# A two-layer encoder kernel: when layer two's skewed position bias is written, how layer one's down-projection ends, and how layer two's values start

## The chip, the cores and the metric

The kernel runs on one core of one Trainium2 chip. The metric is the device time of one execution in microseconds. Three runs of the kernel before the change took 2891.97, 2894.02 and 2900.52 us; their median, 2894.02, is the time before. One more execution was profiled.

## The reference, cut to what matters

There are 1024 prompt rows and 8 x 16 sample rows of width 1024: 1152 rows, nine token tiles of 128. Two layers follow each other, each an attention and a gated feed-forward network with a causal convolution. Layer one looks back two chunks of 64, with a T5 bias and sinks. Layer two looks back eight chunks; its keys and values come from layer one's output, and its bias is a table by clipped distance.

```python
def relclip_bias(table, qpos, kpos):
    d = jnp.clip(qpos[:, None] - kpos[None, :], -REL_CLIP, REL_CLIP) + REL_CLIP
    return table[:, d]

def conv_ffn(h, prev, w_up, conv_w, conv_b, w_down):
    u = h @ w_up
    ...
    a, g = jnp.split(y, 2, axis=-1)
    out = (jax.nn.gelu(g) * a) @ w_down
    return out, ue[:, T:]
...
        x = layer_norm(ALPHA * x + (1 + g_f) * f, ln_g[l, 1], ln_b[l, 1])
        if l == N_A_LAYERS - 1:
            kv = ((x * (1 + sc_kv) + sh_kv) @ w_kv_b).reshape(B, T, 2, N_HEADS_B, HEAD_DIM)
            k_b = kv[:, :, 0]
            v_b = kv[:, :, 1]
```

## The kernel before, in words

Every product is done as three matmuls of high and low halves. `wload` (L174 to L180) loads a weight tile of 128 x 1024 into a staging buffer of the ring `self.ws`, and `split` makes the two halves: ScalarE casts the high one (L161), GpSimd or VectorE subtracts for the low one (L172). They land in a slot of `self.wring`.

The order of the work in `build` is: `opening` (first modulation, first hidden rows, half of layer one's keys), `tables` (layer one's bias table, written to `ea`), `attention(0)`, `out_proj(0)`, `ffn(0)`, `attention(1)`, `out_proj(1)`, `ffn(1)`. The program is one stream; a scheduler puts each engine's instructions in an order by its own simulated times and the order in the text, and each engine then runs its queue strictly in that order. All transfers are issued by SyncE.

**The skewed bias.** A head's bias depends on the distance only. `skew` (L1339 to L1344) writes each head's table row 128 times behind itself into a buffer in device memory, so that a read with a row pitch one element short gives the shifted rows: `ska`, 3 MB, for layer one and `skb`, 6 MB, for layer two. For layer two, `tables_b` makes the table `eb` (a load, two steps on VectorE, a store) and `skew(1)` copies it in one transfer; both stand at the start of `down` for layer one. `skb` is first read in `attention(1)`.

**Up-projection** (`ffn`). Two pairs of weight tiles go plainly (`plain`); the other twenty through `spair`, seven half-size products per pair (L1188), evicted by ScalarE and VectorE (L1147 to L1155), convolved (`conv_row`, L1027), gated and written to `actD` (L1073 to L1075). In layer one background products (`ada`) run between.

**Down-projection** (`down`). Three groups of three token tiles, `GR = ((0, 1, 2), (6, 7, 8), (3, 4, 5))`. For each of 22 weight tiles `fetch` loads a weight tile and a piece of `actD` and splits both; then 18 matmuls (L1255) add into six banks. In layer one there are four weight slots and five staging buffers, two of which (`lng`, `lnb`) lie where the last gated rows stood. When a group's sums are complete, `evict` (L1268) multiplies them by the gate, and `tail` adds the residual (L1274) and calls `norm_tail`: statistics (L871 to L875), square root (L860), scaling (L902), eight transposes on TensorE (L912) into the banks of `TBG`, their eviction with an affine (L920, L924), a copy of the transposed rows (`zt`, L928) that is written to `hmD`, and the split into `H`, from which the next projections read. In layer two, `KEEP = 6` weight tiles of the last group are kept back and multiplied token tile by token tile, each tile ending by itself; in layer one all three tiles of a group end together.

**Layer two's keys and values** (`attention(1)`). `vproj` makes one quarter of the value columns for all nine tiles in the order `LV[1]`, each tile 24 matmuls (L303) in one of banks 0 to 3 in turn, evicted by ScalarE and VectorE (L353, L354) and written to `vH`. The first quarter comes first, then the keys (`kproj`, L291) with `rescale` between, then the three other quarters, then `load_hm`, which loads the nine tiles of `hmD` into a ring of three buffers (L811), scales them (L815) and splits them into `H` for the queries. The order of the values now:

```python
LV = ((0, 1, 2, 8, 3, 4, 5, 6, 7), (0, 1, 2, 6, 7, 8, 3, 4, 5))
```

`issue_after(ins)` adds an edge of issue order behind `ins`; it is used in `ada` (matmuls behind a matmul) and in `out_proj` (loads behind a load). `keep_in_program_order` pins an instruction behind everything that was traced on its engine before.

Of the kernel before, what the change touches and what calls it, by code (L numbers as in the profile page):

```python
# [16 lines left out]
NT = 9  # L17
# [18 lines left out]
KEEP = 6  # L36
# [10 lines left out]
EL = "p"  # L47
# [50 lines left out]
class Trunk:  # L98
# [187 lines left out]
    def mmT(self, w, out, s0, n):  # L286
        H = self.H
        i = 0
        for a, p in ((1, 0), (0, 1), (0, 0)):
            for k in range(8):  # L290
                self.nc.tensor.matmul(  # L291
                    out[:, 0:n], w[a][:, k * 128 : k * 128 + 128], H[:, p, k, s0 : s0 + n], start=i == 0, stop=i == 23
                )
                i += 1

# [43 lines left out]
    def vproj(self, l, q, banks, tmp):  # L339
        nc = self.nc  # L340
        w = [self.wload(self.I[("wv0", "wv1")[l]][q, i]) for i in range(2)]
        o0 = (896, 512)[l]
        cs = slice(q * 256, q * 256 + 256)
        for t in LV[l]:
            ps = self.bank(banks.next())
            self.mmX(ps, t * 128, w, 4, 256)
            hl, v = tmp.next()
            v = v[:, 0:256]
            ts = slice(t * 128, t * 128 + 128)
            if t < 8:  # L350
                h4 = hl[:, 0:512].rearrange("p (h i d) -> p h i d", i=2, d=64)
                p3 = ps[:, 0:256].rearrange("p (h d) -> p h d", d=64)
                nc.scalar.copy(h4[:, :, 0, :], p3)  # L353
                nc.vector.tensor_sub(h4[:, :, 1, :], p3, h4[:, :, 0, :].bitcast(F32))  # L354
                nc.sync.dma_start(
                    self.vH[l][ts, 4 * q : 4 * q + 4, :], hl[:, 0:512].bitcast(F32).rearrange("p (h d) -> p h d", d=128)
                )
            if t * 128 >= o0:
                nc.scalar.copy(v, ps[:, 0:256])
                nc.sync.dma_start(self.O[("va", "vb")[l]][t * 128 - o0 : t * 128 - o0 + 128, cs], v)  # L360
            if t == 8:
                nc.sync.dma_start(self.vS[l][:, cs], v)


    def attention(self, l, wk):
# [440 lines left out]
    def load_hm(self, ring, aff):  # L806
        nc = self.nc
        G, B = aff
        for t in range(NT):
            s = ring.next()  # L810
            nc.sync.dma_start(s, self.hmD[t])  # L811
# [179 lines left out]
    def ffn(self, l, xsrc, xdst, affs):  # L991
# [222 lines left out]
        for j in range(NPL, NFF):  # L1214
            spair(j)
        self.drain()
# [3 lines left out]
    def down(self, l, xsrc, xdst, affs):  # L1220
# [7 lines left out]
        if l == 0:  # L1228
            self.tables_b(F[:, 1152:3200])
            self.skew(1)  # L1230
# [62 lines left out]
        for gi, g in enumerate(GR):  # L1293
            keep = KEEP if l and gi == 2 else 0
# [36 lines left out]
    def tables_b(self, t):  # L1331
# [5 lines left out]
        nc.sync.dma_start(self.eb, t)  # L1337

# [113 lines left out]
    def build(self):  # L1452
# [4 lines left out]
        self.tables()  # L1457
        self.attention(0, wk)
# [138 lines left out]
```

## Time and profile before

| | |
|---|---|
| median of 3 runs | 2894.02 us (2891.97 to 2900.52) |
| profiled execution, its own time | 2892.5 us |
| its span, first to last instruction | 2890.7 us |
| granted TensorE clock, mean | 0.973 |
| moved by DMA | 471.15 MB, mean 163 GB/s |

How to read it: the profile gives busy time for each engine, the waits of an engine with what ended them, the chain of waits that ended last, and, for any stretch, busy time, granted clock and share of the DMA engines. `L1188` is line 1188 of the kernel before. A row of waits reads: the waiting engine, what it writes and its line, `<-` who ended the wait, then total us, number of waits, the longest. A row of a timeline reads: start, duration, engine, line, operation, output and inputs, count, and in brackets the idle time ahead of it and what ended that. `SPq` is SyncE's queue, where a row is the issue of a transfer and not the transfer itself. PE is TensorE, ACT ScalarE, DVE VectorE, POOL GpSimd.

### The profile page before, as it was taken

How to read it: one execution, taken by the hardware profiler on the slowest of the kernel's cores; microseconds unless marked ns; L12 is line 12 of the kernel's file. 1: busy time of each engine (PE TensorE's matmuls, PEld its weight loads, DVE VectorE, ACT ScalarE, POOL GpSimd, SP SyncE). 2: the span in 40 equal slices, each digit the busy share in tenths (PEclk: the TensorE clock that was granted, in tenths of full speed). 3: DMA queues.
4: the chain of work that ended last, by engine and by line, in shares of the span. 5: the costliest groups of instructions: out<-in, count | busy, mean ns of one | idle time of the engine just before them, and what ended most of it. 6: DMA issues, size and time to landing. Idle time of an engine off the chain costs nothing.

```text
span 2890.7 us, 47351 instructions
## 1 busy us (share of the span) xinstructions
PE 2725.0 (94%) x17734; PEld 2425.9 (84%) x17734; DVE 1805.0 (62%) x3674; ACT 1296.9 (45%) x2613; POOL 1157.0 (40%) x761
## 2 busy tenths in 40 slices
PE   7999899999999959998999899979999999998997
PEld 5887678899999948887899788857899999997886
DVE  4477777876667743562112667767788778884763
ACT  3476634433333333543324666653454444453442
POOL 2122424444444435655731121232354443447662
PEclk8999899999999979999999899989999999999999
DMA  8655454434444374664865356675432222247561
GB/s 298 207 164 167 134 176 164 159 133 156 141 143 139 129 228 168 232 212 161 279 230 177 106 150 177 173 234 165 153 133 69 85 72 77 69 146 231 200 210 70
DMA packets 221062, 471.15 MB, mean 163 GB/s; under 512 B 39616, under 2 KB 115600, under 8 KB 220832
## 3 DMA queue, kind: packets, MB, share of 16 engines
q1 hardware_dynamic: 220832, 468.13, 49.5%
q8 instruction: 139, 2.28, 0.3%
q14 instruction: 91, 0.75, 0.1%
HBM read 366.74 MB, written 110.74 MB: 165 GB/s over the span
## 4 chain that ended last, share of the span: by engine, by line
PE 80%; DMA 8%; DVE 5%; ACT 3%; issue 2%; POOL 2%; SPq 0%; POOLq 0%; DVEq 0%; ACTq 0%
PE PS L1188 31%; PE PS L1255 17%; PE PS L291 11%; PE PS L303 10%; PE PS L587 2%; PE PS L565 2%; PE PS L218 2%; PE PS L537 1%; PE PS L540 1%; DMA actD<-F 1%; DMA F<-in_wdn_dram 1%; DMA ws<-in_wo_dram 1%; DVE F L504 1%; PE PS L912 1%; POOL H L172 1%
## 5 line engine op out<-in xcount | busy, mean ns | idle before, releaser
L1255 PE MATMUL PS<-wh,xa 128*128 128x512 f32 x1128 | 359.0, 397 | 40.6 <-ACT wh L161 40.6
L1188 PE MATMUL PS<-H,wh 128*128 128x256 f32 (+1 forms) x2560 | 394.2, 296 | 0.0
L1188 PEld LDWEIGHTS PS<-H,wh 128*128 128x128 f32 x2560 | 360.3, 190 | 0.0
L1248 DVE TENSOR_TENSOR xa<-xa 128x384 fp32r<-128x384 f32 x132 | 185.7, 1419 | 238.0 <-ACT xa L161 238.0
L172 POOL TENSOR_TENSOR wl<-ws,wh 128x1024 fp32r<-128x1024 f32 x87 | 216.8, 2495 | 291.5 <-ACT wh L161 277.5
L161 ACT CAST wh<-F 128x512 fp32r<-128x512 f32 (+1 forms) x249 | 176.0, 713 | 347.4 <-PE PS L1188 139.7
L1150 DVE TENSOR_TENSOR F<-PS,F 128x320 f32<-128x320 f32 (+2 forms) x600 | 192.5, 351 | 164.7 <-PE PS L1188 161.3
L291 PE MATMUL PS<-H,wh 128*128 128x384 f32 (+1 forms) x1536 | 294.8, 338 | 0.0
L1255 PEld LDWEIGHTS PS<-wh,xa 128*128 128x128 f32 x1128 | 213.3, 189 | 93.5 <-ACT wh L161 41.5
L291 PEld LDWEIGHTS PS<-H,wh 128*128 128x128 f32 x1536 | 267.4, 188 | 1.5 <-issue 1.0
L161 ACT CAST wh<-ws 128x1024 fp32r<-128x1024 f32 (+1 forms) x175 | 146.8, 843 | 247.9 <-PE PS L1188 99.7
L1027 DVE SCALAR_TENSOR_TENSOR F<-F 128x1024 f32<-128x1024 f32 x320 | 249.7, 822 | 6.4 <-ACT F L1066 5.3
L1188 PE MATMUL PS<-H,wl 128*128 128x256 f32 (+1 forms) x1280 | 228.1, 298 | 5.2 <-ACT F L1155 5.2
L172 DVE TENSOR_TENSOR wl<-F,wh 128x512 fp32r<-128x512 f32 x196 | 196.8, 1012 | 46.2 <-ACT wh L161 45.6
L1255 PE MATMUL PS<-wl,xa 128*128 128x512 f32 x564 | 224.8, 399 | 0.2 <-POOL wl L172 0.2
L1188 PEld LDWEIGHTS PS<-H,wl 128*128 128x128 f32 x1280 | 189.4, 190 | 12.2 <-issue 5.8
L1188 PE MATMUL PS<-xa,wh 128*128 128x256 f32 (+1 forms) x1280 | 196.1, 295 | 0.6 <-DVE xa L172 0.6
L303 PE MATMUL PS<-wh,H 128*128 128x256 f32 (+1 forms) x936 | 171.3, 313 | 11.2 <-DVE H L172 4.0
L1036 POOL TENSOR_TENSOR F<-F 128x16 f32<-128x16 f32 x88 | 45.1, 513 | 339.6 <-DVE F L1027 256.7
L1188 PEld LDWEIGHTS PS<-xa,wh 128*128 128x128 f32 x1280 | 178.7, 188 | 1.4 <-DVE xa L172 1.0
L172 POOL TENSOR_TENSOR wl<-F,wh 128x1024 fp32r<-128x1024 f32 x53 | 130.4, 2463 | 91.7 <-ACT wh L161 89.5
L1255 PE MATMUL PS<-H,xa 128*128 128x512 f32 x684 | 161.6, 395 | 1.9 <-POOL H L172 1.9
(245 smaller groups left out, 5686.3 us busy)
## 6 DMA issues: line engine op xcount, KB each, us to landing
F<-in_wdn_dram SPq DMA_DIRECT2D x71, 512.0 KB
ws<-in_adaw_dram SPq DMA_DIRECT2D x64, 512.0 KB
ws<-in_wdn_dram SPq DMA_DIRECT2D x61, 512.0 KB
ws<-in_wup_dram SPq DMA_DIRECT2D x50, 512.0 KB
actD<-F SPq DMA_DIRECT2D x44, 576.0 KB
xa<-actD SPq DMA_DIRECT2D x132, 192.0 KB
F<-in_adaw_dram SPq DMA_DIRECT2D x48, 512.0 KB
F<-in_wup_dram SPq DMA_DIRECT2D x38, 512.0 KB
```

The lines of the kernel that those rows point to most:

```text
L161: nc.scalar.copy(out, in_)
L172: self.eng(el).tensor_sub(lo, src, hi.bitcast(F32))
L218: mm = nc.tensor.matmul(ps[32 * j : 32 * j + 32, hf * 256 : hf * 256 + 256], self.cT[:, k * 32 : k * 32 + 32], w[:, j * 256 : j * 256 + 25 ...
L291: self.nc.tensor.matmul(out[:, 0:n], w[a][:, k * 128 : k * 128 + 128], H[:, p, k, s0 : s0 + n], start=i == 0, stop=i == 23)
L303: self.nc.tensor.matmul(out[:, 0:n], H[:, p, j * kn + k, t0 : t0 + 128], w[a][:, k * n : k * n + n], start=i == 0, stop=i == 23,)
L565: nc.tensor.transpose(t[:, n * 128 : n * 128 + 128], p[:, (kt - k0) * 128 : (kt - k0) * 128 + 128], self.ident)
L587: mm = nc.tensor.matmul(ob[:, i0 * 128 : (i0 + n) * 128], vst[a][:, kt, :], pp[:, m * 128 : (m + n) * 128], start=cnt == 0, stop=cnt == to ...
L1027: nc.vector.scalar_tensor_tensor(o, u, cw[:, cc, i : i + 1], o, op0=ALU.mult, op1=ALU.add)
L1150: nc.vector.tensor_add(d, o, x)
L1188: nc.tensor.matmul(ps[:, 0:m], w[a][:, k * 128 : k * 128 + 128], x(p, k, n), start=start and c == 0, stop=c == 11, skip_group_check=True,)
L1248: nc.vector.tensor_sub(lo, raw, hi.bitcast(F32))
L1255: nc.tensor.matmul(ps, a[p][:, i * 128 : i * 128 + 128], w[q][:, hf * 512 : hf * 512 + 512], start=j == 0 and c == 0, stop=j == NFF - 1 an ...
```

## The change

1. `tables_b` is called in `build` right behind `tables`, ahead of `attention(0)`, in another buffer. `skew(1)` is gone; a new function `skew_b` copies one head, and `ffn` calls it behind each of the first sixteen `spair`s of layer one.
2. In `down`, `KEEP` becomes `(4, 6)`: layer one too keeps weight tiles of its last group back, four of them. It gets two more weight slots, in `X2`; in its last group the transposed rows go to `zt` and `lnb` in turn, and the scaled rows to `hf` and `F[:, 0:1024]` in turn.
3. `vproj` takes several quarters and a cut: it loads all their weights, then makes the tiles of `LV` ahead of the cut for each quarter, then the tiles behind it. Layer two starts with quarters 0 and 1 and a cut of six (tiles 0, 1, 2, 6, 7, 8 first); quarters 2 and 3 follow the keys.
4. `mmT` remembers its last matmul, and `load_hm` issues its loads inside `issue_after` of it.

```diff
-KEEP = 6
+KEEP = (4, 6)
...
@@ mmT
-                self.nc.tensor.matmul(
+                mm = self.nc.tensor.matmul(
...
+        self.lastmm = mm.ins
@@ vproj (the body of the loop over tiles becomes vtile)
+    def vproj(self, l, qs, banks, tmp, cut=NT):
+        ws = [[self.wload(self.I[("wv0", "wv1")[l]][q, i]) for i in range(2)] for q in qs]
+        for part in (LV[l][:cut], LV[l][cut:]):
+            for q, w in zip(qs, ws):
+                for t in part:
+                    self.vtile(l, q, t, w, banks, tmp)
@@ attention
-        self.vproj(l, 0, kvb, kvt)
         if l == 0:
+            self.vproj(0, (0,), kvb, kvt)
             self.skew(0)
         else:
+            self.vproj(1, (0, 1), kvb, kvt, 6)
...
-            for q in range(1, 4):
-                self.vproj(1, q, kvb, kvt)
+            self.vproj(1, (2,), kvb, kvt)
+            self.vproj(1, (3,), kvb, kvt)
@@ load_hm
-            nc.sync.dma_start(s, self.hmD[t])
+            with self.tc.issue_after(self.lastmm):
+                nc.sync.dma_start(s, self.hmD[t])
@@ ffn
         for j in range(NPL, NFF):
             spair(j)
+            if l == 0 and 2 <= j < 18:
+                self.skew_b(j - 2)
@@ down
-        if l == 0:
-            self.tables_b(F[:, 1152:3200])
-            self.skew(1)
...
-        if l:
+        if l == 0:
+            order += [(self.X2[:, o : o + 1024], self.X2[:, o + 1024 : o + 2048]) for o in (0, 2048)]
+        else:
...
-        hfr = Ring([self.hf])
+        hfr, hfe, zts = Ring([self.hf]), Ring([self.hf, F[:, 0:1024]]), Ring([self.zt, self.lnb])
...
-                self.norm_tail(t, row, xdst, aff, True, Ring(TBG[gi]), "a", None, None, hfr, EL, VA)
+                if gi == 2:
+                    self.zt = zts.next()
+                self.norm_tail(t, row, xdst, aff, True, Ring(TBG[gi]), "a", None, None, (hfr, hfr, hfe)[gi], EL, VA)
...
-            keep = KEEP if l and gi == 2 else 0
+            keep = KEEP[l] if gi == 2 else 0
@@ skew_b (new)
+    def skew_b(self, h):
+        src = self.eb[h : h + 1, :]
+        self.nc.sync.dma_start(
+            self.skb[h : h + 1, :].rearrange("h (q w) -> h q w", w=768),
+            bass.AP(src.tensor, src.offset, [[768, 1], [0, 128], [1, 768]]),
+        )
@@ build
         self.tables()
+        self.tables_b(self.F[:, 8192:9472])
         self.attention(0, wk)
```

More of the change, by code (lines that the diff above doesn't have):

```diff
@@ L342, in vproj @@
         o0 = (896, 512)[l]
         cs = slice(q * 256, q * 256 + 256)
[L344 to L362, printed above, removed]
+        ps = self.bank(banks.next())
@@ new lines, in vtile @@
+        self.mmX(ps, t * 128, w, 4, 256)
+        hl, v = tmp.next()
+        v = v[:, 0:256]
+        ts = slice(t * 128, t * 128 + 128)
+        if t < 8:
+            h4 = hl[:, 0:512].rearrange("p (h i d) -> p h i d", i=2, d=64)
+            p3 = ps[:, 0:256].rearrange("p (h d) -> p h d", d=64)
+            nc.scalar.copy(h4[:, :, 0, :], p3)
+            nc.vector.tensor_sub(h4[:, :, 1, :], p3, h4[:, :, 0, :].bitcast(F32))
+            nc.sync.dma_start(
+                self.vH[l][ts, 4 * q : 4 * q + 4, :], hl[:, 0:512].bitcast(F32).rearrange("p (h d) -> p h d", d=128)
+            )
```

9 lines of the change are left out of this document (7 added, 2 removed).

## The prediction

> **What bounds the kernel now.** I read the page first, then the waits of TensorE over the whole span, then the chain of waits, and last the timelines of the two stages that the change touches.
>
> ```profile
> span 2890.7 us, 47351 instructions
> PE 2725.0 (94%) x17734; PEld 2425.9 (84%) x17734; DVE 1805.0 (62%) x3674; ACT 1296.9 (45%) x2613; POOL 1157.0 (40%) x761
> PE 80%; DMA 8%; DVE 5%; ACT 3%; issue 2%; POOL 2%; SPq 0%; POOLq 0%; DVEq 0%; ACTq 0%
> ```
>
> TensorE is busy for 2725.0 of 2890.7 us, and the change removes no matmul. What it can win lies in the 165.7 us in which TensorE stands still, and in matmuls run at a lower clock. So I looked for TensorE's single long waits.
>
> ```profile
> PE PS L1255 <- ACT wh L161: 40.6, 2, 33.4
> ```
>
> ```profile
> PE PS L912 <- ACT F L928: 8.9, 1, 8.9
> PE PS L912 <- DVE F L902: 5.2, 1, 5.2
> PE PS L303 <- POOL H L172: 3.2, 2, 2.1
> ```
>
> The first row (whole span) has one wait of 33.4 us, at the start of layer one's down-projection. The three others are all that TensorE waits for between 1330 and 1400 us, the seam between layer one's down-projection and layer two's value projection: 17.3 us. Together 50.7 us, and both places are edited.
>
> Why the 33.4 us: the issue queue of SyncE, the size of one transfer in the DMA list, and SyncE's own waits.
>
> ```profile
> 1047.40 0.60 SPq L1342 DMA_DIRECT2D skb<-eb  x1
> 1048.13 6.88 SPq L1075 DMA_DIRECT2D actD<-F  x1
> ...
> 1071.72 14.12 SPq L176 DMA_DIRECT2D F<-in_wdn_dram  x3
> ```
>
> ```profile
> skb<-eb SPq DMA_DIRECT2D x1, 6144.0 KB
> ```
>
> ```profile
> SPq L176 <- DMA actD<-F: 9.4, 1, 9.4
> ```
>
> At 1047.40 the skewed bias of layer two goes out as one transfer of 6144 KB. The last gated activation is issued right behind it, and the fourth and fifth weight tile may be loaded only when that write has left its buffer: at 1071.72. So the copy takes about 1071.7 - 1048.1 = 23.6 us, and TensorE waits for all of it and the loads behind.
>
> **The change part by part.**
>
> *The copy leaves the down-projection.* What is then late is the same chain without the copy: gate, write of the activation, weight load, cast. Layer two runs this stage without such a copy, and this is all that TensorE waits for from 2580 us to the end:
>
> ```profile
> PE PS L1255 <- ACT wh L161: 7.2, 1, 7.2
> PE PS L1255 <- POOL H L172: 1.9, 1, 1.9
> PE PS L1255 <- POOL wl L172: 0.2, 1, 0.2
> ```
>
> I take 7.2 + 1.9 = 9.1 us for what stays: gain 33.4 - 9.1 = 24.3 us. Ends: 29 (two more weight slots shorten the chain) and 17 (the residue nearly doubles). The stall also leaves TensorE slow behind it:
>
> ```profile
> 1048.00:1072.00 24.00, 1.65 (x8) 0.99 (x6) 2.66 (x2) 1.56 (x2) 5.32 (x3) 0.61 0.98 315
> 1072.00:1084.00 12.00, 0.91 (x2) 0.81 (x3) 0.56 (x1) 2.38 (x3) 0.89 (x1) 0.50 0.77 224
> 1084.00:1100.00 16.00, 16.00 (x63) 12.70 (x63) 4.90 (x2) 4.35 (x7) 9.53 (x5) 0.89 0.45 152
> ```
>
> ```profile
> 1083.09 98.36 PE PS L1255 x412
> ...
> 1197.60 78.87 PE PS L1255 x338
> ```
>
> In the windows the last three columns are granted clock, DMA share and GB/s: the clock is 0.50 in the stall and 0.89 in the 16 us behind it. In the chain the 412 matmuls behind the stall take 98.36/412 = 0.2387 us each, later ones 78.87/338 = 0.2333: 412 x 0.0054 = 2.2 us, gone with a short stall. Ends 1 and 3.
>
> *The seam (17.3 us).* Today all three tiles of the last group end together. Value tiles and the end's transposes share accumulator banks 0 and 1, so only value tiles in banks 2 and 3 may go first, and of these only two need none of the three ending tiles. Then TensorE stands behind transposes whose evictions stand behind something else:
>
> ```profile
> 1361.59 0.82 SPq L811 DMA_DIRECT2D F<-hmD  x2
> ```
>
> ```profile
> 1368.66 3.18 ACT L815 ACTIVATE F<-F,C 128x128 f32<-128x128 f32 x8 [5.61 <-DMA F<-hmD]
> 1371.75 0.28 ACT L860 ACTIVATE C<-C 128x1 f32<-128x1 f32 x2
> 1371.93 3.17 ACT L815 ACTIVATE F<-F,C 128x128 f32<-128x128 f32 x8
> ```
>
> ```profile
> 1387.59 8.89 PE PS L303 x72
> ```
>
> ScalarE's in-order queue holds the scaling of two tiles loaded far ahead (L815), and waits 5.61 us for their load while the square roots (L860) that the end needs stand behind it. The change answers in three ways. (a) Four weight tiles are kept back and each token tile ends by itself: 24 matmuls x 0.2333 = 5.6 us apart, so two of the three ends run while TensorE still multiplies. (b) Two column quarters start together: by the ring of four banks six value tiles lie in banks 2 and 3, not two, and a value tile is 24 matmuls, 8.89/3 = 2.96 us: 17.8 us of cover in place of 5.9. (c) The loads of L811 are placed inside an order edge behind the last key matmul. I count (c) as nothing: as I read it, the edge binds only instructions of that matmul's own engine, and these are loads on SyncE; every use in the kernel today pairs instructions of one engine. So the 5.61 us wait and 2 x 3.2 us of scaling may still stand ahead of the last tile's evictions. Today the first transposes start 5.9 + 5.2 = 11.1 us behind the last matmul, with three tiles sharing VectorE; for the last tile alone I estimate 8. L815 can add 5.61 + 2 x 3.2 = 12: 20 us against 17.8 us of cover leaves 2, and I add 2 for transposes queued a little early. I take 4 of 17.3: gain 13. Ends 16 and 7. Keeping weights back: layer two already keeps six, and the rows above hold no wait for it; 0, bound 3. The first two value weights are split later than now, since their slots carry kept tiles until the last token tile: 1 us, the 1.9 us row being the nearest bound.
>
> *Where the copy goes.* It is traced inside the up-projection, one head (1/16 of 6144 KB, 23.6/16 = 1.5 us) per pair of weight tiles. But each piece depends only on the small table, which is now built in the opening, and this schedule issues what is ready:
>
> ```profile
> L993 SPq DMA_DIRECT2D F<-in_cw_dram x2: 383/460/537, 257.0 to 1824.5; - x2
> ```
>
> ```profile
> 485.39 10.88 PE PS L291 x62
> ```
>
> The convolution weights are the first statement of this very up-projection, whose first matmuls start at 485.39, and they are issued at 257.0, as soon as their buffer is free. The pieces need no buffer. I expect all 16 right behind the table, from about 60 us, where layer one's twin of this copy stands today (last fence of the rivals). There the DMA engines look so (windows from 60 us):
>
> ```profile
> 60.00:75.00 15.00, 12.73 (x104) 12.52 (x102) 0.85 (x2) 2.44 (x5) 2.40 (x1) 1.00 1.03 351
> 75.00:85.00 10.00, 8.48 (x58) 8.49 (x59) 1.70 (x4) 2.81 (x6) 2.37 (x1) 0.83 0.60 210
> 85.00:95.00 10.00, 10.00 (x79) 10.00 (x79) 1.70 (x4) 1.86 (x5) 0.00 (x0) 1.00 0.98 290
> 95.00:106.00 11.00, 11.00 (x65) 11.00 (x64) 2.22 (x4) 2.73 (x7) 0.58 (x4) 1.00 0.83 223
> 106.00:140.00 34.00, 32.57 (x251) 28.09 (x249) 20.78 (x69) 20.88 (x65) 5.33 (x7) 1.00 0.49 156
> ```
>
> ```profile
> 76.52 0.78 PE L303 MATMUL PS<-wh,H 128*128 128x256 f32 x4 [3.79 <-DVE X L354]
> ...
> 106.21 0.22 PE L537 MATMUL PS<-xa 128*128 128x128 f32 x1
> ```
>
> Layer one's own bias copy fills 60 to 75 us, and already costs TensorE 3.79 us, through key writes queued behind it. Up to 106 us, when layer one's scores begin, the free part of the DMA engines is 10 x 0.40 + 10 x 0.02 + 11 x 0.17 = 6.1 us. If all 23.6 us of pieces run ahead of the keys, values and queries that the scores need, these come 23.6 - 6.1 = 17.5 us later, and TensorE has nothing else to do. Bounds: 0 if the pieces fall behind the start, where half of 34 us is free; 24 if they lead entirely. Some will slip behind the start, so I take 15. The table's two DVE steps and two small transfers join the opening; they are inside this bound.
>
> If the pieces do stay in the up-projection they cost nothing: TensorE's waits from 535 to 1000 us are 4 us in all, none on a transfer, the longest being
>
> ```profile
> PE PS L1188 <- ACT F L1155: 2.3, 1, 2.3
> ```
>
> *Sum*, on the profiled execution (2892.5 us): -24.3 - 2.2 - 13 + 1 + 15 = -23.5: 2869.0. That execution lies 1.5 us under the median of the runs (2894.0), so 2870.5 for the median, told as 2870.
>
> **The rivals.** *The pieces cost little* (under 8 us): the scheduler keeps them behind the keys and values, or where they are written. For it: 17 us of DMA time are free between 106 and 140 us, and the order of issue favours earlier program text among what is ready. Against: L993's 257.0. Sum with 0: 2854.0, 2855.5 for the median.
>
> *Slower: the pieces land one by one ahead of layer one's first keys.* A small write from the table's twin shows how long one landing takes:
>
> ```profile
> 55.41 0.33 SPq L1329 DMA_DIRECT2D ea<-F  x1
> ```
>
> ```profile
> 59.06 0.85 SPq L1342 DMA_DIRECT2D ska<-ea  x1
> ```
>
> The copy at 59.06 waits for the table issued at 55.41: 3.65 us. Sixteen such landings, each awaited before the next, are 58 us in place of 23.6; less the 6.1 us of room, 52. Against it: the order of issue runs several transfers deep. With the other terms as above the sum is 2892.5 - 38.5 + 52 = 2906, and 2907.5 for the median. It decides for slower once the opening loses over 38.5 + 8.7 = 47 us. The Trainium skill, page "DMA: Bandwidth & Descriptors", section "Anatomy of one DMA", speaks against cutting a copy up: each DMA on the GpSimd path pays some 2.0 us besides its bytes over 436 GB/s, by which an estimate for 16 pieces is 16 x 2.9 = 46 us, 40 less the room, and a total of about 2895; the page states this for another path than SyncE's, and no run here shows it yet.
>
> *Nothing to see*: the seam's ends slip behind the early scaling all the same (gain 7 or less), the residue nearly doubles (gain 17) and the opening pays 24: 2892.5 - 17 - 1 - 7 + 24 + 1 = 2892.5, 2894 for the median.
>
> **How the numbers follow.** Chances: forecast 0.60, little cost 0.24, slower 0.08, nothing to see 0.08. A measurement of this kernel can tell about 0.3%, 8.7 us. Of the forecast's 0.60, opening and seam both near their bad ends (-38.5 + 24 + 6) leave under 8.7 us in about 0.08; so faster 0.76 (0.52 + 0.24), same 0.15, slower 0.09, the last from the slower case and a little of the third. The range reaches down past the cheap case, 2853, and up to where the opening pays 24 and the seam gives 7: 2892.5 - 24.3 - 2.2 - 7 + 1 + 24 + 1.5 = 2885.5, told as 2887.
>
> **What would show it.** Right: in the changed profile the copy is 16 issues of skb from one line, the last well before 257 us; TensorE's first scores (L537) come 10 to 20 us later than 106; TensorE's longest wait in layer one's down-projection is 5 to 14 us; between the last down-projection matmul and the keys TensorE waits under 7 us in all, the loads of hmD still early. Wrong: the 16 issues lie between 535 and 1000 us, or the first scores come as before (then the cheap case); a wait over 17 us remains at the start of the down-projection though the copy is gone, which would mean that the activation write and not the copy was the cause; or the seam keeps a wait of 9 us on L928.

## The result, and the profile after

The changed kernel takes 2885.70 us (median of 11 runs, 2880.89 to 2890.38); the kernel before took 2895.64 us in the runs beside it (11 runs, 2888.97 to 2901.74). The ratio is 0.9966, with a 95% interval of 0.9953 to 0.998: some 10 us faster. The forecast was 24 us. The time lies inside the range, close to its upper end.

The profiled execution spans 2885.9 us. The longest wait of TensorE over the whole span:

```profile
PE PS L1264 <- ACT wh L161: 25.9, 2, 18.7
```

The line numbers have moved: L1255 is now L1264, L303 is L304, L537 is L544, L1188 is L1196, L912 is L920, L1074 is L1082, L354 is L360, L504 is L511, L811 is L819, L928 is L936. In the kernels of the experiments they move by another line or two. The wait of 33.4 us at the start of layer one's down-projection has become 18.7, not 9.1; the rest of the 25.9 is layer two's, as before.

The seam (all waits of TensorE from 1330 to 1400 us) has 6.2 us where 17.3 stood:

```profile
PE PS L920 <- DVE C L881: 3.2, 1, 3.2
PE PS L920 <- ACT F L936: 2.7, 2, 1.7
PE PS L304 <- DVE X L360: 0.3, 1, 0.3
```

The pieces of the skewed bias went out in the opening, between 68.8 and 117.5 us (one row by tile, then SyncE's issue queue, then TensorE):

```profile
L1352 SPq DMA_DIRECT2D skb<-eb x16: 470/602/2400, 68.8 to 117.5; - x16
```

```profile
82.55 1.78 SPq L1352 DMA_DIRECT2D skb<-eb  x3
84.44 0.53 SPq L361 DMA_DIRECT2D vH<-X  x1
85.02 5.89 SPq L1352 DMA_DIRECT2D skb<-eb  x7
```

```profile
83.52 0.80 PE L304 MATMUL PS<-wh,H 128*128 128x256 f32 x2 [5.39 <-DVE X L360]
...
114.06 0.28 PE L544 MATMUL PS<-xa 128*128 128x256 f32 x1
```

```profile
505.64 10.88 PE PS L291 x62
```

The first scores come at 114.06 in place of 106.21, and the up-projection's first chain at 505.64 in place of 485.39: the 7.9 us lost by the first scores have grown to 20.3.

For all kernels below I read the same milestones in the timeline of TensorE: the first scores, the first and last matmul of layer one's pair tiles, the last matmul of its down-projection, layer two's first scores, the first and last of its pair tiles, the last matmul. Stage lengths in us:

| kernel | to first scores | attention 1 to pairs | pairs 1 | down 1 | seam, keys, values | attention 2 to pairs | pairs 2 | down 2 |
|---|---|---|---|---|---|---|---|---|
| before | 106.2 | 428.5 | 502.3 | 318.1 | 239.8 | 538.2 | 454.0 | 288.8 |
| before, second profile | 106.2 | 430.7 | 503.2 | 318.8 | 237.7 | 545.9 | 455.6 | 289.3 |
| after | 114.1 | 440.9 | 504.3 | 302.8 | 224.9 | 541.1 | 455.4 | 287.6 |
| after, second profile | 118.8 | 435.0 | 501.5 | 303.3 | 226.3 | 540.8 | 455.8 | 287.7 |
| move_only | 117.1 | 438.0 | 501.7 | 302.6 | 237.9 | 539.1 | 456.6 | 286.7 |
| move_again | 116.0 | 445.6 | 504.4 | 301.1 | 235.2 | 534.6 | 453.1 | 287.8 |
| seam_only | 104.5 | 430.7 | 501.0 | 324.2 | 226.0 | 541.5 | 454.8 | 288.3 |
| stage | 119.7 | 436.4 | 503.5 | 282.5 | 223.8 | 541.5 | 453.9 | 288.0 |
| pin | 106.7 | 438.0 | 507.2 | 303.0 | 225.3 | 538.7 | 454.2 | 287.7 |
| late_table | 106.2 | 433.7 | 511.1 | 303.5 | 226.0 | 537.1 | 454.5 | 288.7 |
| whole | 132.1 | 434.2 | 503.9 | 303.9 | 226.8 | 541.7 | 455.3 | 287.4 |
| keep0 | 118.8 | 442.0 | 502.8 | 302.7 | 228.2 | 541.3 | 455.4 | 287.9 |
| one_quarter | 115.0 | 444.2 | 501.9 | 304.1 | 229.0 | 535.7 | 455.0 | 287.5 |
| held | 114.3 | 448.2 | 502.0 | 305.3 | 246.3 | 543.2 | 455.0 | 287.7 |
| pin_stage | 109.6 | 429.1 | 507.2 | 282.5 | 227.5 | 541.3 | 455.4 | 291.7 |
| pin_stage2 | 107.3 | 426.8 | 509.1 | 282.6 | 227.3 | 538.8 | 454.1 | 277.2 |
| pin_down | 108.4 | 429.1 | 504.6 | 290.8 | 225.9 | 538.3 | 453.2 | 277.5 |

In the three kernels with two profiles, the pair tiles and the down-projections mostly repeat within 2 us and always within 3.5. The two attentions don't: the two profiles of the kernel before differ by 7.7 us in layer two's attention alone, with the same instructions. A difference of a few us there is not told by one profile.

### The profile page after: what moved, and what is told of

Same layout as the page of the kernel before. It is cut to its first block, busy times and chain, and to the rows that moved or that the text cites. A ratio compares the mean times of both kernels' runs of the same rounds, so it can differ in the third digit from the quotient of the medians.

```text
span 2885.9 us, 47364 instructions
## 1 busy us (share of the span) xinstructions
PE 2728.5 (95%) x17734; PEld 2425.8 (84%) x17734; DVE 1816.1 (63%) x3674; ACT 1295.1 (45%) x2613; POOL 1159.7 (40%) x761
## 4 chain that ended last, share of the span: by engine, by line
PE 77%; DMA 9%; DVE 6%; issue 3%; ACT 2%; POOL 2%; SPq 1%; POOLq 0%; DVEq 0%; ACTq 0%
PE PS L1196 31%; PE PS L1264 18%; PE PS L291 10%; PE PS L304 8%; PE PS L594 2%; PE PS L572 2%; PE PS L218 2%; PE PS L544 1%; DMA ws<-in_adaw_dram 1%; DVE F L511 1%; PE PS L547 1%; DMA F<-in_adaw_dram 1%; PE PS L920 1%; PE PS L713 1%; DMA skb<-eb 1%
## 5 line engine op out<-in xcount | busy, mean ns | idle before, releaser
L1196 PE MATMUL PS<-H,wh 128*128 128x256 f32 (+1 forms) x2560 | 396.0, 297 | 0.0
L1196 PEld LDWEIGHTS PS<-H,wh 128*128 128x128 f32 x2560 | 362.2, 191 | 0.0
L172 POOL TENSOR_TENSOR wl<-ws,wh 128x1024 fp32r<-128x1024 f32 x78 | 193.6, 2487 | 313.7 <-ACT wh L161 302.1
L161 ACT CAST wh<-F 128x512 fp32r<-128x512 f32 (+1 forms) x236 | 162.4, 694 | 332.3 <-PE PS L1196 144.6
L1264 PE MATMUL PS<-wh,xa 128*128 128x512 f32 x864 | 279.2, 400 | 25.9 <-ACT wh L161 25.9
L291 PE MATMUL PS<-H,wh 128*128 128x384 f32 (+1 forms) x1536 | 294.4, 337 | 0.0
L291 PEld LDWEIGHTS PS<-H,wh 128*128 128x128 f32 x1536 | 267.2, 188 | 1.4 <-issue 0.6
L161 ACT CAST wh<-ws 128x1024 fp32r<-128x1024 f32 (+1 forms) x166 | 137.4, 831 | 238.8 <-PE PS L1196 97.6
L1196 PE MATMUL PS<-H,wl 128*128 128x256 f32 (+1 forms) x1280 | 229.1, 299 | 5.2 <-ACT F L1163 5.2
L1264 PEld LDWEIGHTS PS<-wh,xa 128*128 128x128 f32 x864 | 164.1, 190 | 66.5 <-ACT wh L161 26.8
L1196 PEld LDWEIGHTS PS<-H,wl 128*128 128x128 f32 x1280 | 190.1, 191 | 12.2 <-ACT F L1163 5.6
L1196 PE MATMUL PS<-xa,wh 128*128 128x256 f32 (+1 forms) x1280 | 196.1, 295 | 0.6 <-DVE xa L172 0.6
L304 PE MATMUL PS<-wh,H 128*128 128x256 f32 (+1 forms) x936 | 171.9, 314 | 11.1 <-DVE X L360 5.7
L1196 PEld LDWEIGHTS PS<-xa,wh 128*128 128x128 f32 x1280 | 178.6, 188 | 1.4 <-DVE xa L172 1.0
L1264 PE MATMUL PS<-wl,xa 128*128 128x512 f32 x432 | 171.9, 398 | 0.2 <-POOL wl L172 0.2
L291 PE MATMUL PS<-H,wl 128*128 128x384 f32 (+1 forms) x768 | 156.3, 345 | 6.6 <-DVE xa L498 2.7
L1264 PE MATMUL PS<-H,xa 128*128 128x512 f32 x684 | 161.1, 395 | 0.0
```

The lines of the kernel that those rows point to most:

```text
L161: nc.scalar.copy(out, in_)
L172: self.eng(el).tensor_sub(lo, src, hi.bitcast(F32))
L291: mm = self.nc.tensor.matmul(out[:, 0:n], w[a][:, k * 128 : k * 128 + 128], H[:, p, k, s0 : s0 + n], start=i == 0, stop=i == 23)
L304: self.nc.tensor.matmul(out[:, 0:n], H[:, p, j * kn + k, t0 : t0 + 128], w[a][:, k * n : k * n + n], start=i == 0, stop=i == 23,)
L1196: nc.tensor.matmul(ps[:, 0:m], w[a][:, k * 128 : k * 128 + 128], x(p, k, n), start=start and c == 0, stop=c == 11, skip_group_check=True,)
L1264: nc.tensor.matmul(ps, a[p][:, i * 128 : i * 128 + 128], w[q][:, hf * 512 : hf * 512 + 512], start=j == 0 and c == 0, stop=j == NFF - 1 an ...
```

## The experiments

**The pieces held where they are written (pin).** Each piece is queued on SyncE behind the activation store that was traced just before it.

```diff
 def skew_b(self, h):
-    self.nc.sync.dma_start(...)
+    d = self.nc.sync.dma_start(...)
+    self.tc.keep_in_program_order(d)
```

> The changed kernel with one edit: each of the 16 pieces of the skewed bias is queued on SyncE behind the store of the activation written just before it, so it can't float ahead of the up-projection; the small table stays in the opening. Theory A (the floating pieces are the loss: first scores at 114.06 us in place of 106.21, first L291 chain of the up-projection at 505.64 in place of 485.39): both go back to 106 +- 1 and 486 +- 3, the up-projection from 535 to 1040 hides the pieces, and the time is 2885.7 - 20 = 2866 (2860 to 2872). Rival B (the table's steps and the changed order of the value helper slow the opening and the first attention, not the pieces): first scores stay near 114, the first L291 chain near 505, time 2883 to 2888. Rival C (the pieces cost wherever they lie, 23.6 us of transfer): the time stays within 5 us of 2886, with the loss moved into the up-projection.

Ratio to the kernel before 0.9915 (0.9901 to 0.9929), 2873.57 us, against 0.9966 for the changed kernel. The pieces now lie in the up-projection, and the first scores are back:

```profile
L1352 SPq DMA_DIRECT2D skb<-eb x16: 476/477/1533, 584.8 to 968.1; - x16
```

```profile
106.73 0.22 PE L544 MATMUL PS<-xa 128*128 128x128 f32 x1
```

Theory A holds for the first scores, not for the rest: the first L291 chain comes at 495.44, not at 486, since the attention stage still took 438.0 us in this profile, and the pair tiles took 507.2, so the up-projection does not hide the pieces. (Applied to 2895.64, the ratio gives 2871, at the upper end of its range.) Rival C has part of it. SyncE and GpSimd around one piece show what the pair tiles lose (the pair's second weight load is the row at 740.15; GpSimd works on it at 746.38):

```profile
739.58 0.48 SPq L1352 DMA_DIRECT2D skb<-eb  x1
740.15 0.83 SPq L1142 DMA_DIRECT2D ws<-in_wup_dram  x1
```

```profile
746.38 1.30 POOL L1145 TENSOR_TENSOR F<-ws 128x512 f32<-128x512 f32 x1 [7.21 <-DMA ws<-in_wup_dram]
```

The weights queued behind the piece need 6.2 us from issue to use; in the changed kernel, with no piece there, the same load needs 3.6 (749.35 to 752.91). TensorE has a gap of 1.2 us at 759.5, one of three small gaps there that the profiles of before and after do not have; the gap ends on an eviction by ScalarE, so a link from the late weights to it is likely, but not shown. Pieces in the up-projection are not free either.

**The first part alone (move_only, and again as move_again on another chip).** Table in the opening and pieces in `ffn`, on the kernel before; no kept tiles, no added slots, values as before.

> The kernel before with only the first part of the change: table in the opening, 16 pieces written in the up-projection (free to float), nothing of the seam, no kept tiles, no added weight slots. Theory A: +20 before the up-projection, and a wait of some 19 us where 33.4 us stood, 2895.6 + 20 - 15 = 2901 (2896 to 2905): this part alone costs time or gives nothing. Rival (the sum of the prediction: -24.3 - 2.2 + 15): 2884. Rival D (the pieces cost only the 8 us by which the first scores slip, and the 12 us lost later in the first attention come from elsewhere in the change): first L291 chain at 493, 2889.

> The kernel before with only the table in the opening and the 16 pieces free to float, once more on another chip. By stages: +17 up to the up-projection (four profiles with floating pieces against eight without), -16 at the start of the down-projection: theory A 0.999 to 1.002 of the kernel before. Rival (the first timing, 0.9966 with 0.9951 to 0.9981, is what this part is worth, and the profiles of the kernel before are luckier than its timed runs): 0.995 to 0.998.

The ratios are 0.9966 (0.9951 to 0.9981) and 0.9974 (0.9963 to 0.9984): 8 to 10 us faster, so theory A missed both times, and a rival came nearer. By stages against the two profiles of before it loses 10.4 to the first scores and 12.2 in the attention, and wins 16.6 in the down-projection, where waits of 14.9 and 15.2 are left. These three make +6, the timed runs -8 to -10. The two profiled spans of this kernel (2894.4 and 2892.6 us) are longer than its medians (2890.71 and 2889.02), and the attentions differ between profiles by as much, so the two counts can't be brought together closer than this: how much is left when the opening's loss is set against the stall's gain stays open.

**The seam alone (seam_only).** The changed kernel with table and copy put back at the start of `down`.

```diff
-            if l == 0 and 2 <= j < 18:
-                self.skew_b(j - 2)
...
+        if l == 0:
+            self.tables_b(F[:, 1152:3200])
+            self.skew(1)
```

> The changed kernel with the copy put back into the down-projection as one transfer, its table with it; kept tiles, the two added weight slots, the tiles' ends one by one and the value quarters stay. Theory A (the seam is worth 15 us, by the stage times 239.0 against 224.0 us): 2895.6 - 15 = 2881 (2876 to 2886), and TensorE's wait at the start of the down-projection is 30 to 35 us as before. Rival E (most of the seam's gain comes from the copy being gone from the queue): 2890 or more. Rival F (the two added slots shorten that wait by themselves): wait under 25 us, time under 2875.

Ratio 0.9964 (0.995 to 0.9978). The seam takes 226.0 us, as in the changed kernel: that gain stands by itself. The wait at the start of the down-projection is even longer with the copy there:

```profile
PE PS L1265 <- ACT wh L161: 39.1, 1, 39.1
```

so the two added slots shorten nothing, and this took 6 of the 13 us of the seam back. Beside the changed kernel (0.9966) this run also says what moving the copy is worth once the seam is changed: nothing that can be told. By stages the down-projection gets 21 us shorter, and the opening and the attention 19 longer.

**The staging slots (stage).** The changed kernel; layer one's first six weight tiles of the down-projection go through the two `ws` slots and `F[:, 0:1024]` alone.

```diff
-        self.ws = Ring(narrow.items + [F[:, 0:1024]] + ([self.hf] if l else [self.lng, self.lnb]))
+        early = (narrow.items + [F[:, 0:1024]]) * 2
+        late = narrow.items + [F[:, 0:1024]] + ([self.hf] if l else [self.lng, self.lnb])
+        self.ws = Ring(late * 20 if l else early + late * 20)
```

> The changed kernel with one edit: layer one's first six down-projection weight tiles are staged only through the two ws slots and F[0:1024]; the slots lng and lnb, which lie over the buffer (F from 10492 on) of the last gated activation, come in from the seventh tile on. Theory G (the 18.7 us that are left are the fourth and fifth weight tile waiting for that buffer: its GpSimd product ends at 1074.8, its store frees it, and only then the loads of 1077.46 and 1078.19 go out): the longest wait there is 0 to 6 us and the time 2885.7 - 15 = 2871 (2866 to 2876). Rival H (the wait is transfer bandwidth or the splits on GpSimd, which come as late from any slot): wait 14 us or more, time over 2881.

Ratio 0.9891 (0.9876 to 0.9906), 2867.88 us: by the ratios 22 us under the changed kernel, and the wait is gone. TensorE in the 30 us behind the last pair tile (last columns: granted clock, DMA share, GB/s):

```profile
1059.70:1075.00 15.30, 15.30 (x67) 12.31 (x66) 14.06 (x14) 9.17 (x13) 11.09 (x6) 1.00 0.56 178
1075.00:1090.00 15.00, 15.00 (x66) 12.08 (x65) 1.78 (x1) 1.36 (x3) 8.95 (x4) 1.00 0.86 198
```

Theory G holds: the 18.7 us were two weight tiles that could not be loaded because their staging slots lay over the last gated activation. The stage fell by more than that, from 303 to 282.5.

**One transfer in place of 16 (whole).** The changed kernel with `skew(1)` behind the table in the opening, and no pieces.

> The changed kernel with the 16 pieces put together again into one transfer of 6144 KB that depends on the table in the opening alone. Theory A (the opening pays for bytes on shared transfer engines, 23.6 us of them, not for the number of transfers): first scores between 112 and 124 us, first pair tile of the up-projection at 552 to 560, time within 5 us of the changed kernel, 0.995 to 0.998 of the kernel before. Rival (each of the 16 transfers pays a start of its own, some 2 us by the Trainium skill's page on DMA): 15 x 2 = 30 us less work for the queue, first scores before 110, 0.990 or less.

Ratio 1.0017 (1.0008 to 1.0027): 15 us slower than with pieces. Neither side named this. The first scores come at 132.1 us. SyncE's queue, ScalarE's wait, TensorE:

```profile
70.03 0.95 SPq L1358 DMA_DIRECT2D skb<-eb  x1
71.09 16.92 SPq L329 DMA_DIRECT2D kH<-X  x1
```

```profile
ACT X L359 <- DMA kH<-X: 17.6, 1, 17.6
```

```profile
103.00 0.58 PE L304 MATMUL PS<-wh,H 128*128 128x256 f32 x1 [23.90 <-DVE X L360]
```

The issue of a write of keys takes 16.9 us behind the big transfer in the queue; the values are evicted through the same buffers, and TensorE waits 23.9 us for that eviction. The pieces leave gaps in which keys and values get through (the write of `vH` at 84.44 above stands between two batches of them): cutting the copy up saved 15 us of a loss that the move itself made. The Trainium skill, page "DMA: Bandwidth & Descriptors", section "Anatomy of one DMA", gives each DMA on the GpSimd path a fixed 2.0 us; on SyncE here three pieces were issued in 1.78 us and the cut was worth it, so for this queue that price does not decide.

**The changed kernel again (after_again), and the table moved too (late_table).** The second is pin with `tables_b` called at the start of layer one's up-projection.

> The changed kernel unedited, to have it on the same chip as the kernels beside it, and a second profile of it. Theory A (the pieces cost 8 to 13 us up to the first scores; the 10 to 12 us more up to the up-projection belong to where half-clock stretches of TensorE fall, 3.41 us or a multiple each, and change from execution to execution): first scores at 112 to 120 us again, but the distance from there to the first pair tile of the up-projection, 440.9 us in the first profile, comes out different by several us; wait at the down-projection's start 17 to 20. Rival (a fixed cost of this order of instructions): that distance is 441 +- 2. Time 0.994 to 0.998 of the kernel before.

> The changed kernel with the pieces queued behind the activation stores, and its small table built at the start of layer one's up-projection in place of the opening: all of layer two's bias work leaves the opening. Theory A (the table itself costs nothing; the 10 us which the kernel with only the pieces queued lost in the first attention were half-clock stretches of that execution): within 4 us of that kernel, 0.990 to 0.993 of the kernel before. Rival B (the table's two VectorE steps and two transfers disturb the first attention): 8 to 12 us faster than that kernel, 0.987 to 0.989, and the first pair tile of the up-projection at 535 in place of 545.

Ratios 0.9963 (0.9951 to 0.9975) and 0.9923 (0.9908 to 0.9937). The table in the opening costs nothing that can be told: late_table is no faster than pin. The attention stage took 435.0 in the second profile of the changed kernel, against 440.9; with nothing floating it lay between 426.8 and 438.0. Over the eight profiles with floating pieces (move_only, move_again, both of after, keep0, one_quarter, held, stage) the first scores come at 116.7 on average and the attention takes 441.3; over the eight without (both of before, seam_only, pin, late_table, pin_stage, pin_stage2, pin_down) 106.9 and 430.8. The pieces cost 9.8 + 10.5 = 20.3 us. The timed runs agree: pin is 15 us under the changed kernel by the ratios (0.9915 against 0.9966), though its pair tiles are some 6 us longer.

**Parts of the seam (keep0, one_quarter, held), and before again.** keep0 has `KEEP = (0, 6)`; one_quarter calls `vproj` for quarter 0 and then for quarter 1; held queues each load of `hmD` behind everything traced on SyncE before.

> The changed kernel with no weight tile kept back for layer one's last group: its three token tiles end together again, while the two value quarters stay together. The stage from the last down-projection matmul to layer two's first scores took 239.8 us before and 224.8 and 226.3 in two profiles of the changed kernel. Theory S (the cover by six value tiles carries most of the gain): 225 to 230. Rival (the ends one by one carry it): 234 to 240, with a wait of 5 us or more on L936 or L910 as before.

> The changed kernel with the value quarters one after the other, all nine tiles of the first before the second, and kept tiles and single ends as changed: only two value tiles can run in banks 2 and 3 before the transposes. Theory S: the last ending tile finds 5.9 us of cover in place of 17.8, and the stage from the last down-projection matmul to layer two's first scores takes 233 to 240 us. Rival (ends one by one carry the gain): 225 to 229.

> The changed kernel with the nine loads of hmD queued behind everything traced before them on SyncE itself (in the changed kernel their order edge names a TensorE matmul; two of them went out at 1365.04, as early as before). Theory (ScalarE's early scaling at 1372 to 1381 us is what the last token tile's evictions stand behind): the waits of 3.2, 1.7 and 1.0 us in the seam fall to 2 us in all, the stage to layer two's first scores takes 220 to 223 us in place of 224.8 and 226.3. Rival (held loads come late at the other end): the first scores wait for H on ScalarE more than the 2.2 and 6.7 us of now, and the stage takes 226 to 235.

> The kernel before, unedited, for a second profile of it. The kernel with only the pieces moved was some 10 us faster than the kernel before in timed runs, but 3.7 us longer by the two profiles. Theory V (the wait at the start of the down-projection differs between executions, 33.4 us in the first profile, 39.1 in the kernel with only the seam changed, and the first profile is a lucky one): wait 36 to 42, down-projection from last pair tile to last matmul 321 to 327 in place of 318.1. Rival: all stages within 2 us of the first profile, and the difference stays open.

keep0 takes 228.2 and one_quarter 229.0 us in this stage; before 238.7 on average, with both parts 225.6. Each part alone brings some 10 us, the other only 3 more, from one profile each; the ten profiles with both parts lie between 223.8 and 227.5. So theory S held in keep0 and missed in one_quarter, where it named 233 to 240. The longest waits of TensorE in this stage, in keep0

```profile
PE PS L304 <- DVE X L360: 5.7, 2, 5.4
```

and in one_quarter:

```profile
PE PS L921 <- DVE C L882: 3.2, 1, 3.2
PE PS L304 <- DVE X L360: 3.2, 1, 3.2
```

The rows of 8.9 and 5.2 us of before are in neither. With the loads really held, the 2.7 us on L936 went and a far longer wait came (stage 246.3, 2918.54 us in its one run, against 2904.66 for before):

```profile
PE PS L291 <- ACT H L161: 22.7, 2, 22.0
```

The second profile of the kernel before has 33.7 us where 33.4 stood, and 237.7 in the seam: theory V is wrong, that profile was not lucky there.

**The two edits together (pin_stage, pin_stage2), and pieces in the down-projection (pin_down).** pin_stage is pin and stage in one. pin_stage2 uses `early` in layer two too. pin_down is pin_stage2 with the pieces queued behind the loads of the seventh to 22nd weight tile of the first group:

```diff
                 w, a = fetch(j, g[0])
+                if l == 0 and gi == 0 and j >= 6:
+                    self.skew_b(j - 6)
```

> Both edits in one: pieces queued behind the activation stores, and layer one's first six weight tiles staged through the two ws slots and F[0:1024] alone. Theory (the two losses, in the opening and at the start of the down-projection, lie 900 us apart and add up): -24.6 and -31.5 + 9.9 us beside the kernel before, -46 in all: 0.982 to 0.986. Rival (the pieces queued in the up-projection delay the early weight loads, and part of the wait comes back): wait over 4 us at the start of the down-projection, and 0.987 or more.

> The kernel with both edits, and the same order of staging slots in layer two's down-projection too (its fourth slot, F[4224:5248], lies over a buffer that the last convolution still reads). Theory G (layer two's 7.1 us wait is the same thing, a staging slot that lies over a live buffer; it was taken in the prediction as the residue that any such start has): the wait falls under 2 us, and the time is 6 to 9 us under the kernel without this edit, 0.980 to 0.983. Rival (7.1 us is what gate, store, load and cast need in any case): no change.

> The kernel with staging slots in the free order in both layers, but with the 16 pieces queued behind the activation loads of the seventh to 22nd weight tile of layer one's first down-projection group, in place of the up-projection's pairs. Theory W (in the up-projection a piece delays the pair's own weights, 6.2 us from issue to landing behind it, and four pairs lose 1.2 us each; in the down-projection six tiles are fetched ahead and cover it): up-projection pairs 501 to 504 us in place of 507 to 511, down-projection from last pair tile to last matmul 281 to 284 as without pieces, 0.979 to 0.982 of the kernel before. Rival (the bytes cost the same wherever they lie): the down-projection grows by 4 us or more.

pin_stage: 0.9866 (0.985 to 0.9883), 39 us in place of 46; its down-projection is as short as in stage, and its pair tiles take 507.2, as in pin. pin_stage2: 0.9819 (0.9805 to 0.9833), 2844.59 against 2899.32 us, 55 us under before. Layer two's waits of pin_stage

```profile
PE PS L1266 <- ACT wh L161: 7.6, 1, 7.6
PE PS L1266 <- POOL H L172: 1.9, 1, 1.9
```

are gone in pin_stage2, where no wait is left from 2546 us to the end. The stage fell from between 286.7 and 291.7, in all profiles without this edit, to 277.2: the 9.1 us that the prediction took for the residue of any such start were the same kind of collision, a staging slot over a buffer still in use. pin_down: 0.9805 (0.9787 to 0.9823), no different. Its pair tiles take 504.6, but its down-projection 290.8 in place of 282.6, with two new waits there:

```profile
PE PS L1264 <- POOL wl L172: 2.1, 1, 2.1
PE PS L1264 <- ACT wh L161: 2.0, 1, 2.0
```

The rival holds: the pieces cost 4 to 8 us in either place.

## Why the prediction was off

By its own terms, in stages (means of two profiles each, before and after):

| term | predicted | measured | |
|---|---|---|---|
| copy leaves the down-projection, and the clock behind it | -24.3 - 2.2 | -15.4 | 318.5 to 303.1 |
| pieces in the opening | +15 | +20.3 | eight profiles against eight |
| seam, with later value weights | -13 + 1 | -13.1 | 238.7 to 225.6 |
| sum | -23.5 | -8.2 | timed: -10 (0.9953 to 0.998) |

**The step that failed is the residue.** "Layer two runs this stage without such a copy", so 9.1 us stay: the analogy took a wait without its cause. It measured 18.7: a gain of 14.7, under the lower end of 17. This term alone is 11 of the 15 us by which the sum of the stages was off. The chain of waits after has the cause, and the word that gave it stood in the text ahead of the prediction: `lng` and `lnb` lie where the last gated rows stood.

```profile
1071.89 2.94 POOL F L1082
...
1074.85 3.28 DMA actD<-F
...
1078.19 11.29 DMA F<-in_wdn_dram
...
1089.57 1.05 ACT wh L161
...
1090.66 97.77 PE PS L1264 x412
```

Read downward: GpSimd's product (L1082), the store that frees the buffer, the load into it, ScalarE's cast, TensorE. Ahead of the product GpSimd did a weight split, of a tile other than the one that TensorE lacked:

```profile
1069.53 2.41 POOL L172 TENSOR_TENSOR wl<-ws,wh 128x1024 fp32r<-128x1024 f32 x1
```

The kernel before had most of this in its rows (the product, and the store from the chain):

```profile
1045.37 2.74 POOL L1074 TENSOR_TENSOR F<-F 128x1152 f32<-128x1152 f32 x1
```

```profile
1048.13 23.53 DMA actD<-F
```

Product from 1045.37, 2.74 us; a store, 3.3 as now in place of 23.5; and from the issue of the load (1071.72) to TensorE's restart (1083.09) 11.4. That ends at 1062.8, 13 us behind TensorE's stop at 1049.7: so the copy was 20 of the 33.4 us, and the links that remain gave 13, where another layer's row gave 9. The other 5.6 us came new: the product starts where TensorE stops, not 4.3 us ahead of it, and from load to restart are 12.5 us.

Most of these 5.6 us go with the two added weight slots, which the prediction's better end of 29 counted as a help. The split ahead of the product stands in every profile with the added slots and the old staging order; without the copy, their waits are 17.4 to 19.0 us (18.5 in keep0, which keeps no tile back). In move_only and move_again, without the slots, the product goes first and the waits are 14.9 and 15.2. In move_only, where TensorE stopped at 1069.3:

```profile
1065.35 2.69 POOL L1074 TENSOR_TENSOR F<-F 128x1152 f32<-128x1152 f32 x1
1067.98 5.31 POOL L172 TENSOR_TENSOR wl<-ws,wh 128x1024 fp32r<-128x1024 f32 x2
```

No run adds the slots alone, so this is a comparison of kernels that differ in more than the slots. The prediction's own sign for a wrong step, a wait over 17 us, came true. Its reading, the write and not the copy, is half right: the copy lengthened the write, and the slots made the write matter.

**The clock behind the stall** was put at 2.2 us; the chain's 412 matmuls take 97.77 in place of 98.36 us: 0.6, since a wait of 18.7 us lowers the clock as well (granted clock 0.63 in the wait, and 0.92 from 1091 to 1107, where 0.89 stood).

**The pieces** did what was said: right behind the table and far ahead of 257 us, none between 535 and 1000. The 15 us were expected at the first scores; half of the cost came there (+7.9 and +12.6 in the two profiles, where 10 to 20 was the sign) and half later. What makes the second half was not isolated, but two rows of TensorE's waits in the attention go with it. One is the wait for the modulation's weights; five pieces went out only at 113 to 117.5 us. The row of before, of after, and of whole:

```profile
PE PS L218 <- DMA ws<-in_adaw_dram: 4.3, 5, 1.4
```

```profile
PE PS L218 <- DMA ws<-in_adaw_dram: 10.5, 9, 2.6
```

```profile
PE PS L218 <- DMA ws<-in_adaw_dram: 4.3, 9, 0.6
```

It is 7.4 to 14.7 us in the eight profiles with floating pieces, and 2.7 to 4.3 in the eight without, except for pin, which has 8.2 and the longest attention of these. The other row is scores that wait for VectorE's step of the softmax (L511), and so for no transfer: 5.6 to 7.3 us in the eight, at most 1.0 in the eight without. In after:

```profile
PE PS L544 <- DVE F L511: 5.6, 8, 1.4
```

With the single transfer, which was out before the scores, this row has 3.2 us and the attention took 434.2, less than the 441.3 with pieces. **"If the pieces do stay in the up-projection they cost nothing"** was wrong by some 6 us (508.7 on average in the four profiles with pieces there, 502.7 in the twelve with none of them there or behind): no wait of TensorE's named a transfer there, but a weight load behind a piece needed 6.2 us in place of 3.6, as pin showed.

**The seam** was right in size, and its signs came true: waits under 7 us (6.2), the loads of `hmD` as early as before (an edge behind a TensorE matmul does not hold a load on SyncE back),

```profile
1365.04 0.80 SPq L819 DMA_DIRECT2D F<-hmD  x2
```

and no wait of 9 us on ScalarE's copies. But the size came out right in part by luck. The sum set 20 us for the last token tile's end against six value tiles of cover, 17.8 us. TensorE's rows behind its last down-projection matmul (1362.15), the second and third tile's transposes:

```profile
1371.99 1.07 PE L920 MATMUL PS<-C,F 128*128 128x128 f32 x8 [3.22 <-DVE C L881]
1377.65 0.66 PE L920 MATMUL PS<-C,F 128*128 128x128 f32 x4 [1.73 <-ACT F L936]
```

The last tile's transposes start after 15.5 us, not 20, and the timeline has 72 value matmuls ahead of them: three value tiles, not six. Both figures were too large, and since one was taken from the other, the two errors nearly cancelled. One_quarter too has three value tiles there, which fits its keeping most of the gain: (a) and (b) cover in part the same waits. That the edge does nothing turned out well: with the loads held behind everything on SyncE, the stage is 21 us longer.

The time still lies inside the range, but not for the range's reasons: its upper end was worked out from a seam of 7 us and an opening that pays 24, with the copy's gain in full. Of the rivals, "the pieces cost little" fell with pin and whole. "Nothing to see" had the copy's gain (17) and the opening's cost (24) nearly right, and the seam (7) wrong. "Slower" got its mechanism in another form: a transfer in front of the first keys, but one big one (whole), not many small ones.

## What to carry to other kernels

When a long wait has a chain of links, price what is left of that chain link by link after the cut; another stage's wait is a bound only if it has the same links, and the buffers that staging slots lie over are links. Added slots can lengthen a wait, as they seem to have done here: they let later work stand ahead of the link that is waited for. In a schedule like this one, a transfer that depends on nothing goes out when it is ready, not where it is written: pin it, or expect it in the busiest place, and cut it up if others must pass. Two edits that cover the same wait are worth little more than one.

## What the runs showed of the hardware

**A short gap can cost more than its length.** TensorE's clock fell to half for stretches of 3.4 us and multiples of it. In pin a gap of 1.87 us ended at 131.62 (four windows of 3.4 us; the first numbers are TensorE's busy time, the third from last the clock):

```profile
127.70:131.10 3.40, 1.95 (x16) 1.11 (x15) 3.31 (x11) 3.33 (x11) 1.01 (x1) 0.99 0.76 223
131.10:134.50 3.40, 2.88 (x16) 2.07 (x17) 1.33 (x6) 1.36 (x6) 0.54 (x3) 0.50 0.56 167
134.50:137.90 3.40, 3.40 (x12) 3.40 (x11) 0.00 (x0) 0.00 (x0) 0.00 (x0) 0.50 0.54 191
137.90:141.30 3.40, 3.40 (x26) 3.35 (x26) 1.35 (x6) 1.50 (x4) 0.00 (x0) 1.00 0.16 39
```

The same wait in the kernel before was 1.32 us, and the clock stayed:

```profile
128.40:131.90 3.50, 2.07 (x19) 1.27 (x18) 3.40 (x11) 3.42 (x12) 1.27 (x1) 1.00 0.82 283
```

Two windows at half clock behind a gap half a microsecond longer: ahead of it pin's scores come 0.5 us later than those of before, behind it 3.9. The Trainium skill, page "TensorE: Matmul & The Clock Gate", section "What's actually happening", says that a free-running window of 3413 ns decides on half or full clock; the stretches agree with that length, and a window in which TensorE was still busy for 1.95 of 3.40 us was enough here. It fits that the two attentions, full of such gaps, differ by up to 7.7 us between profiles of one kernel, and the chains by less; that the phase of the window makes that difference was not shown.

**A stall takes more than its wait with it.** In layer one, stage removed a wait of 18.7 us (17.8 in the second profile of the changed kernel) and shortened the down-projection by 20.5, with the granted clock at 1.00 throughout, where 0.63 had stood in the wait. Removing layer two's 7.6 and 1.9 us shortened its stage by 14.5 us from pin_stage to pin_stage2 (by 9 to 12 against the others); there too the clock was 0.50 behind the last pair tile, and 1.00 throughout without the stall:

```profile
2568.00:2578.00 10.00, 5.06 (x11) 3.57 (x12) 7.55 (x4) 3.46 (x4) 10.00 (x4) 0.50 0.63 211
```

```profile
2562.00:2572.00 10.00, 10.00 (x44) 8.06 (x43) 6.83 (x5) 3.82 (x5) 10.00 (x5) 1.00 0.83 273
```
